# Starting the parts of x and the later tiles 64 bytes off the weights in each SBUF partition

## The chip, the cores and the metric

The kernel runs on one core of a Trainium2 chip. The metric is the device time of one execution in microseconds. The kernel before took 2917.8 us (median of 3 runs, 2917.19 to 2920.89).

## The reference, cut to what matters

The reference is a float32 transformer of two stacks of two layers on 512 tokens of 1024 features. Each layer mixes tokens in its own way, and most of the arithmetic is the dense products around the mixing:

```python
def first_block(x, mem, ...):
    for layer in range(DEPTH):            # 2
        mix = even_mixer(x, ...) or odd_mixer(x, ...)   # mLSTM + neighbourhood attention, differential attention
        x = layer_norm(DEEPNORM_ALPHA * x + mix, ...)
        xa = memory_cross_attention(x, mem, ...)        # 256 memory tokens
        x = layer_norm(DEEPNORM_ALPHA * x + xa, ...)
        ff = swiglu(x, ffn_w_gu[layer], ffn_w_down[layer])
        x = layer_norm(DEEPNORM_ALPHA * x + ff, ...)
    return x
```

The second stack has two more layers of mixer (HGRN2 and forgetting attention, RG-LRU and stick-breaking attention), layer norm, SwiGLU, layer norm. The hidden width of a SwiGLU is 2816.

## The kernel before

x is kept feature-major: 8 tiles of 128 features by 512 tokens. Every dense product is done in float32 accuracy with single-pass `float32r` matmuls: each operand is cut into a high and a low part that add up to it, and the product is the sum of three matmuls (high by high, low by high, high by low), `mm3`, lines 274 to 276. A matmul of TensorE has a stationary operand of 128 by 128, which a LDWEIGHTS brings in, and a moving operand whose columns stream past it. In this kernel every matmul has a weight load of its own.

`fetch` (from line 327) loads a block of weights of 128 by 1024 into `w_raw`, and ScalarE (line 337) and VectorE (line 339) make `w_hi` and `w_lo` of it. `block_a` multiplies such a block, as stationary operand, with the parts of x (`xh`, `xl`) or of the hidden units (`f_h`, `f_l`) as moving operand, 512 or 256 columns wide. `proj_b` does it the other way round: the parts of x are stationary and 512 columns of the weights move. `close_sublayer` ends a sublayer in two halves of 256 tokens, so its matmuls are 256 columns wide, and it keeps four of its eight blocks of weights in a pool of its own, `cw`. `mem_kv` makes keys and values of the memory: for the keys the parts of the memory (`mm_h`, `mm_l`, 256 columns) move past the weights, for the values 512 columns of the weights move past the parts of the memory.

The order of the instructions on each engine is set by the program and its scheduler. Where a tile lies is set by pools: a pool opened later begins where the one before it ends, each tile behind the other, in bytes of each of the 128 partitions; pools of the right side (those of the memory, `mem` and `kv`) grow from the top. The constants end with a tile of 16 bytes and with others that put everything behind them 32 bytes behind a multiple of 128; all big tiles are multiples of 128 bytes (most of 2048 or 4096), so that nearly everything on the left side begins at 32 (mod 128).

Of the kernel before, what the change touches and what calls it, by code (L numbers as in the profile page):

```python
# [8 lines left out]
F32 = mybir.dt.float32  # L9
# [7 lines left out]
P = 128  # L17
# [11 lines left out]
# last layer norm: tiles that GpSimd subtracts from and multiplies, that VectorE ends, and how they are stored  # L29
# [24 lines left out]
def layout(i):  # L54
    """Lays the inputs out for the loads of the program; values are copied, never changed."""
# [25 lines left out]
    # neighbourhood bias, per kind of query tile: [head, query, kind, key]; keys outside the window are shut out  # L81
# [125 lines left out]
class Prog:  # L207
    def __init__(self, ctx, tc, a):
        self.tc, self.nc, self.a = tc, tc.nc, a
        nc = tc.nc  # L210
        self.cp = ctx.enter_context(tc.tile_pool(name="cst", bufs=1))
        self.st = ctx.enter_context(tc.tile_pool(name="state", bufs=1))
        self.wp = ctx.enter_context(tc.tile_pool(name="wts", bufs=4))
        self.ps = ctx.enter_context(tc.tile_pool(name="ps", bufs=4, space=PSUM))
        st = self.st
        xf = st.tile([P, KT * S], F32, name="xf")
        self.XF = [xf[:, k * S : (k + 1) * S] for k in range(KT)]
        self.all_x = xf.rearrange("p (k s) -> p k s", k=KT)
        self.XH = [st.tile([P, S], F32R, name=f"xh{k}") for k in range(KT)]
        self.XL = [st.tile([P, S], F32R, name=f"xl{k}") for k in range(KT)]  # L220
        self.AO = [st.tile([P, S], F32, name=f"ao{k}") for k in range(KT)]
        cp = self.cp

        ones = cp.tile([P, 2 * P], F32, name="k_ones")
        nc.vector.memset(ones[:, 0:P], 1.0 / D)
        nc.vector.memset(ones[:, P : 2 * P], 1.0 / P)
        self.ones_d, self.ones_p = ones[:, 0:P], ones[:, P : 2 * P]
        nr = cp.tile([P, P], F32R, name="k_nr")
        nc.vector.tensor_scalar(nr, ones[:, P : 2 * P], -float(P), None, ALU.mult)
        self.mones_r = nr  # L230
        pr = cp.tile([P, P], F32R, name="k_pr")
        nc.vector.tensor_copy(pr, ones[:, P : 2 * P])
        self.ones_pr = pr
        cc = cp.tile([P, 4], F32, name="k_cc")
        nc.vector.memset(cc[:, 0:1], LN_EPS)
        nc.vector.memset(cc[:, 1:2], 1.0)
        self.eps, self.one = cc[:, 0:1], cc[:, 1:2]
        self.kv = {}
        self.pending = []
        self.biases = []  # L240
        self.before = []
        self.loaded = False
# [12 lines left out]
    def mm(self, tag="mm"):  # L255
        """A bank of PSUM: mm for projections, sc for scores, tp for what follows them."""
        return self.ps.tile([P, S], F32, name="p_" + tag, tag=tag, bufs={"mm": 2, "sc": 4, "tp": 2}[tag])
# [20 lines left out]
    def pair_parts(self, pool, name, width=S):  # L278
        """Room for the scores of two heads of 64 features, twice: per head q (both its parts over each
        other), the high part of k twice, and its low part beside zeros."""  # L280
        sets = []
        for b in range(2):
            q = [pool.tile([P, S], F32R, name=f"{name}q{b}{j}", bufs=1) for j in range(2)]
            k1 = [pool.tile([P, width], F32R, name=f"{name}h{b}{j}", bufs=1) for j in range(2)]
            k2 = [pool.tile([P, width], F32R, name=f"{name}l{b}{j}", bufs=1) for j in range(2)]
            sets.append((q, k1, k2))
        return sets

    def split_q(self, q, src, scale, view=lambda t: t, source=lambda t: t):
        """q[j] = both parts of scale * (rows of head j); the low one in the rows of the other head."""  # L290
# [9 lines left out]
    def split_k(self, k1, k2, pieces, clear, view=lambda t: t):  # L300
        """The parts of k; pieces: (columns, rows of the pair). clear: the zeros are still to be set."""
# [18 lines left out]
    def mm2(self, out, w, x, start, stop):  # L320
        """Sum of the products of all pairs of operands."""
        pairs = [(a, b) for a in w for b in x]
        for n, (a, b) in enumerate(pairs):
            self.nc.tensor.matmul(out, a, b, start=start and n == 0, stop=stop and n == len(pairs) - 1)  # L324

    def fetch(self, src, n=1024, pool=None):
        """Loads a block of weights and splits it into two parts that add up to it exactly."""
# [14 lines left out]
    def block_a(self, w, ps, xh, xl, c0=0, c1=S, kts=None):  # L342
        """ps[:, c0:c1] = (block of W)^T x for the 128 features of the block."""
# [5 lines left out]
    def proj_a(self, src, evac, halves=False, tags=("mm",)):  # L349
        """Feature-major products for a list of blocks; evac(n, psum, c0, c1)."""  # L350
# [20 lines left out]
    def settle(self, count=None):  # L371
        """What the sublayer before left to be done behind the first products of this one."""
        now = self.pending[:count]
        self.pending = self.pending[len(now) :]
        for f in now:
            f()

    def proj_b(self, src, lhs, ntile, evac, halves=False, banks=None):
        """Token-major products with 512 features; lhs(k, t) gives the parts of x^T of token tile t."""
# [31 lines left out]
    def close_sublayer(self, src, hs, ls, first, ln, last=False, keep=True):  # L411
        """x = layer_norm(alpha x + (rest of the sum)); src: 8 blocks, hs/ls: their inputs.
        keep: all of the blocks stay on chip for the second half of the tokens."""
# [4 lines left out]
        more_w = scope.enter_context(tc.tile_pool(name="cw", bufs=4, reuse_waits="tile")) if keep else None  # L418
        turn = dict.fromkeys("sqxrmt", 0)

        def room(kind):
            """A [128, 256] place in AO, which holds nothing at the end of a sublayer."""
# [5 lines left out]
        def statistics(sm, sq, more=()):  # L428
            """Means and reciprocals of the standard deviations, on all partitions."""
# [111 lines left out]
    def close_mixer(self, src, ln, keep=True):  # L541
        """Output projection of what lies in AO; its parts take the place of those of x."""
# [48 lines left out]
    def mem_kv(self, l, pool):  # L591
        """Keys (feature-major, in two parts) and values (token-major) of the memory."""
# [37 lines left out]
    def normalise(self, p, rs, n):  # L630
        """Divides the n score rows held side by side in p by their sums."""
# [5 lines left out]
    def in_turn(self, n, project, scores, values, between=None, place=0):  # L637
        """Work on n groups of heads, the products for the groups to come before what waits for a softmax.
        place: 0 projects one group ahead; 1 and 2 two groups, before the values or after the scores."""
# [94 lines left out]
    def conv_taps(self, out, xp, w, taps, bias=None):  # L734
        """out[t] = sum_j w[j] xp[t + j] (+ bias)."""
# [8 lines left out]
    def mlstm(self, tp, dp):  # L744
        nc, tc, a = self.nc, self.tc, self.a
        w = a["w_e1"]
        with ExitStack() as ctx:
# [36 lines left out]
            # log_sigmoid(f) = min(f, 0) - ln(1 + exp(-|f|)), its sums along each direction,  # L784
            # and the running maximum of log_i - sums
# [73 lines left out]
            def values(h, gs):  # L859
                hs = slice(h * P, h * P + P)  # L860
                for d in range(2):
                    num = self.mm("sc")
                    # g[i] covers the queries from tile i on, or up to it
# [55 lines left out]
    def neighbour(self, tp, between):  # L919
# [3 lines left out]
        def cr(t):  # L923
            """The tokens of a (row, column) grid, column by column."""
            return t.rearrange("p (r c) -> p c r", r=8)

        with tc.tile_pool(name="na", bufs=2, reuse_waits="tile") as np_:
# [64 lines left out]
            def values(pr, x):  # L992
                v, pp = x
                tabs = []
                for p in pp:
                    # key tiles: columns 0-7 and 56-63, 8-23, 24-39, 40-55
# [32 lines left out]
    def rms_rows(self, pool, o, g, out, gate=None):  # L1029
        """out = o / sqrt(mean over the 128 features of o^2 + eps) * g (* gate)."""  # L1030
# [133 lines left out]
    def hgrn(self, fill):  # L1164
        nc, tc, a = self.nc, self.tc, self.a
        w = a["w_e2"]
        with tc.tile_pool(name="hg", bufs=2, reuse_waits="tile") as hp:
# [11 lines left out]
            # lower bound of the forget gates: first row of the softmax over the layers  # L1179
# [34 lines left out]
            def factors(b, q, k, h):  # L1214
                """Left halves of the blocks of 2h tokens: k decayed up to the middle; right halves: q from there."""
# [18 lines left out]
            for h in range(4):  # L1234
# [14 lines left out]
                for n, hl in enumerate(LEVELS):  # L1249
# [11 lines left out]
                    # the queries are the right halves  # L1261
# [6 lines left out]
                # sums over whole blocks of 128, then 256 tokens for the blocks further off  # L1268
# [26 lines left out]
    def neg_log_sigmoid(self, t, tmp):  # L1295
        """t = ln(1 + exp(-|t|)) - min(t, 0)"""
# [7 lines left out]
    def fox_gates(self, pool, cd):  # L1304
        """Sums of -log(forget gate) over the tokens, per head."""
# [15 lines left out]
    def fox(self, v, cd):  # L1321
        nc, tc, a = self.nc, self.tc, self.a
        w = a["w_e2"]
        with tc.tile_pool(name="fx", bufs=2, reuse_waits="tile") as fp:
# [8 lines left out]
            def scores(pr, x):  # L1333
                q, k1, k2 = x
                pairs = []
                for hh in range(2):
# [5 lines left out]
                    for t in (3, 2, 1, 0):  # L1342
                        ts, n = slice(t * P, t * P + P), t * P + P
                        ps = self.mm("sc")
                        # later queries are done with these keys by now
# [49 lines left out]
    def lru(self):  # L1395
        nc, tc, a = self.nc, self.tc, self.a
        w = a["w_o2"]
        with tc.tile_pool(name="lr", bufs=2, reuse_waits="tile") as lp:
# [6 lines left out]
            # -8 softplus(-lam)  # L1405
# [33 lines left out]
            for n in range(4):  # L1439
                r, i, xc = rr[n], ii[n], xcs[n]  # L1440
                nc.vector.tensor_tensor(xc, xc, i, ALU.mult)
                # 1 - a^2 = tanh(-log a) (1 + a^2)
# [12 lines left out]
    def stick(self):  # L1455
        nc, tc, a = self.nc, self.tc, self.a
        w = a["w_o2"]
        with tc.tile_pool(name="sb", bufs=2, reuse_waits="tile") as sp_:
# [10 lines left out]
            def scores(pr, x):  # L1469
                q, k1, k2 = x  # L1470
                heads = []
                for hh in range(2):
                    ws, parts = {}, {}
                    for i in (3, 2, 1, 0):
# [5 lines left out]
                        # softplus(z) = max(z, 0) + ln(1 + exp(-|z|)), for the keys before the query  # L1480
# [17 lines left out]
            def sums(heads):  # L1498
                for ws, parts in heads:
                    for i in (3, 2, 1, 0):  # L1500
                        # less the sums of softplus over the keys from this one up to the query
# [29 lines left out]
def place_tables(nc):  # L1531
    """Loads, where ScalarE needs another table of functions, the one that serves longest."""
# [59 lines left out]
```

## Time and profile before

| what | value |
|---|---|
| median of 3 runs | 2917.8 us |
| profiled execution, span | 2916.1 us |
| TensorE matmul (PE) busy | 2848.7 us, 98% |
| weight loads (PEld) busy | 2415.8 us, 83% |
| VectorE (DVE) busy | 1697.9 us, 58% |
| ScalarE (ACT) busy | 1274.5 us, 44% |
| GpSimd (POOL) busy | 444.1 us, 15% |

The profiled execution's own time is its span. A matmul's duration in the trace goes from its start to the arrival of its last result, so neighbouring matmuls overlap in it; the time that a matmul costs is the distance from its start to the start of the next one. PEld runs beside PE.

### The profile page before, as it was taken

How to read it: one execution, taken by the hardware profiler on the slowest of the kernel's cores; microseconds unless marked ns; L12 is line 12 of the kernel's file. 1: busy time of each engine (PE TensorE's matmuls, PEld its weight loads, DVE VectorE, ACT ScalarE, POOL GpSimd, SP SyncE). 2: the span in 40 equal slices, each digit the busy share in tenths (PEclk: the TensorE clock that was granted, in tenths of full speed). 3: DMA queues.
4: the chain of work that ended last, by engine and by line, in shares of the span. 5: the costliest groups of instructions: out<-in, count | busy, mean ns of one | idle time of the engine just before them, and what ended most of it. 6: DMA issues, size and time to landing. Idle time of an engine off the chain costs nothing.

```text
span 2916.1 us, 40036 instructions
## 1 busy us (share of the span) xinstructions
PE 2848.7 (98%) x15354; PEld 2415.8 (83%) x15354; DVE 1697.9 (58%) x3148; ACT 1274.5 (44%) x2328; POOL 444.1 (15%) x516
## 2 busy tenths in 40 slices
PE   9979999999999999999999999999999999999998
PEld 7668989888887678898888987798888977988887
DVE  5877756333368888563333767873333769733335
ACT  4545544222356776442222544652222548532223
POOL 0432112000031112030000333230000302300003
PEclk9999999999999999999999999999999999999999
DMA  5232522333233225233332321223332331133331
GB/s 180 76 102 84 160 73 73 101 92 97 88 110 92 66 74 173 59 90 99 94 102 76 110 68 59 87 80 101 95 95 90 94 93 43 59 101 99 96 94 67
DMA packets 83073, 269.08 MB, mean 92 GB/s; under 512 B 10649, under 2 KB 15145, under 8 KB 82881
## 3 DMA queue, kind: packets, MB, share of 16 engines
q1 hardware_dynamic: 81376, 261.49, 29.1%
q0 software_dynamic: 1504, 5.04, 0.5%
q8 instruction: 120, 1.97, 0.3%
q14 instruction: 73, 0.59, 0.1%
HBM read 260.14 MB, written 2.15 MB: 90 GB/s over the span
## 4 chain that ended last, share of the span: by engine, by line
PE 78%; DVE 14%; ACT 4%; issue 3%; DMA 1%; POOL 0%; SPq 0%; DVEq 0%; ACTq 0%; POOLq 0%
PE p_mm L275 14%; PE p_mm L274 13%; PE p_mm L276 13%; PE p_sc L274 10%; PE p_sc L276 10%; PE p_sc L275 9%; DVE w_lo L339 2%; DVE ao L450 2%; PE p_tp L275 1%; PE p_tp L274 1%; PE p_tp L276 1%; DVE ac L742 1%; DVE xl L460 1%; PE p_sc L324 1%; PE p_sc L1254 1%
## 5 line engine op out<-in xcount | busy, mean ns | idle before, releaser
L337 ACT ACTIVATE w_hi<-w_raw 128x1024 fp32r<-128x1024 f32 (+2 forms) x478 | 492.9, 1036 | 1107.7 <-PE p_mm L275 482.5
L339 DVE TENSOR_TENSOR w_lo<-w_raw,w_hi 128x512 fp32r<-128x512 f32 (+2 forms) x956 | 654.2, 713 | 507.6 <-ACT w_hi L337 501.3
L274 PE MATMUL p_mm<-xh,w_hi 128*128 128x512 f32 (+1 forms) x1920 | 688.1, 359 | 7.4 <-ACT w_hi L337 5.0
L275 PE MATMUL p_mm<-xl,w_hi 128*128 128x512 f32 (+1 forms) x1920 | 687.3, 358 | 5.9 <-DVE xl L460 4.0
L276 PE MATMUL p_mm<-xh,w_lo 128*128 128x512 f32 (+1 forms) x1920 | 682.9, 356 | 0.0
L275 PEld LDWEIGHTS p_mm<-xl,w_hi 128*128 128x128 f32 x1920 | 364.6, 190 | 59.4 <-DVE xl L460 6.7
L274 PEld LDWEIGHTS p_mm<-xh,w_hi 128*128 128x128 f32 x1920 | 364.6, 190 | 58.5 <-ACT w_hi L337 5.0
L276 PEld LDWEIGHTS p_mm<-xh,w_lo 128*128 128x128 f32 x1920 | 364.5, 190 | 49.4 <-issue 0.6
L274 PE MATMUL p_sc<-xh,w_hi 128*128 128x512 f32 (+1 forms) x1024 | 359.4, 351 | 0.0
L276 PE MATMUL p_sc<-xh,w_lo 128*128 128x512 f32 (+1 forms) x1024 | 358.6, 350 | 0.8 <-DVE w_lo L339 0.8
L275 PE MATMUL p_sc<-xl,w_hi 128*128 128x512 f32 (+1 forms) x1024 | 358.1, 350 | 0.0
L496 POOL TENSOR_TENSOR ao<-xf 128x256 f32<-128x256 f32 x20 | 19.9, 995 | 1689.0 <-DVE xf L489 1293.9
L568 DVE TENSOR_TENSOR f_s<-f_s,p_sc 128x512 f32<-128x512 f32 x80 | 55.0, 687 | 288.8 <-PE p_sc L276 288.8
L276 PEld LDWEIGHTS p_sc<-xh,w_lo 128*128 128x128 f32 x1024 | 193.7, 189 | 26.2 <-DVE w_lo L339 1.0
L274 PEld LDWEIGHTS p_sc<-xh,w_hi 128*128 128x128 f32 x1024 | 193.7, 189 | 25.7 <-issue 0.4
L275 PEld LDWEIGHTS p_sc<-xl,w_hi 128*128 128x128 f32 x1024 | 193.7, 189 | 25.5 <-issue 0.2
L274 PE MATMUL p_sc<-f_h,w_hi 128*128 128x512 f32 (+1 forms) x464 | 157.5, 339 | 0.0
L276 PE MATMUL p_sc<-f_h,w_lo 128*128 128x512 f32 (+1 forms) x464 | 157.2, 339 | 0.2
L275 PE MATMUL p_mm<-f_l,w_hi 128*128 128x512 f32 (+1 forms) x464 | 157.2, 339 | 0.0
L276 PE MATMUL p_mm<-f_h,w_lo 128*128 128x512 f32 (+1 forms) x464 | 156.8, 338 | 0.0
L274 PE MATMUL p_mm<-f_h,w_hi 128*128 128x512 f32 (+1 forms) x464 | 156.8, 338 | 0.0
L275 PE MATMUL p_sc<-f_l,w_hi 128*128 128x512 f32 (+1 forms) x464 | 156.7, 338 | 0.0
(435 smaller groups left out, 4721.9 us busy)
## 6 DMA issues: line engine op xcount, KB each, us to landing
w_raw<-in_f_gu SPq DMA_DIRECT2D x176, 512.0 KB, 3.5
w_raw<-in_w_e SPq DMA_DIRECT2D x70, 512.0 KB, 3.5
w_raw<-in_w_x SPq DMA_DIRECT2D x64, 512.0 KB, 3.8
w_raw<-in_w_o SPq DMA_DIRECT2D x64, 512.0 KB, 3.7
w_raw<-in_f_d SPq DMA_DIRECT2D x64, 448.0 KB, 3.3
w_raw<-in_f_d SPq DMA_DIRECT2D x32, 512.0 KB, 3.5
r_s<-r_t SPq DMA_DIRECT2D x64, 64.0 KB, 2.0
na_b<-in_na_bias SPq DMA_DIRECT2D x6, 384.0 KB, 2.9
```

What stands on the lines that cost most here:

```text
L274: nc.tensor.matmul(out, wh, xh, start=start, stop=False)
L275: nc.tensor.matmul(out, wh, xl, start=False, stop=False)
L276: self.last = nc.tensor.matmul(out, wl, xh, start=False, stop=stop)
L324: self.nc.tensor.matmul(out, a, b, start=start and n == 0, stop=stop and n == len(pairs) - 1)
L337: nc.scalar.activation(hi[:, :n], raw[:, :n], AF.Copy)
L339: nc.vector.tensor_tensor(lo[:, c], raw[:, c], hi[:, c].bitcast(F32), ALU.subtract)
L450: nc.vector.scalar_tensor_tensor(t, t, g, r, ALU.mult, ALU.mult)
L460: nc.vector.scalar_tensor_tensor(xl, t, b, xh.bitcast(F32), ALU.add, ALU.subtract)
L496: eng.tensor_tensor(sm, self.XF[order[0]][:, c], self.XF[m][:, c], ALU.add)
L568: nc.vector.tensor_tensor(s[:, c], s[:, c], ps[:, c], ALU.mult)
L742: nc.vector.scalar_tensor_tensor(out, xp[:, j : j + S], w[j], out, ALU.mult, ALU.add)
L1254: nc.tensor.matmul(ps[:, c * 64 : c * 64 + 64].rearrange("p (n h) -> p n h", h=hl), x[:, cs], halves(x[:, cs], hl)[1], start=True, stop=True,)
```

## The change

Four tiles of 64 bytes that nothing reads or writes are put between others; besides, comments and docstrings are taken out, which moves the line numbers. Cut to its core:

```diff
         self.wp = ctx.enter_context(tc.tile_pool(name="wts", bufs=4))
         self.ps = ctx.enter_context(tc.tile_pool(name="ps", bufs=4, space=PSUM))
+        ctx.enter_context(tc.tile_pool(name="off", bufs=1)).tile([P, 16], F32, name="pad_p")
         st = self.st
         xf = st.tile([P, KT * S], F32, name="xf")
...
+        st.tile([P, 16], F32, name="pad_x")
         self.XH = [st.tile([P, S], F32R, name=f"xh{k}") for k in range(KT)]
         self.XL = [st.tile([P, S], F32R, name=f"xl{k}") for k in range(KT)]
         self.AO = [st.tile([P, S], F32, name=f"ao{k}") for k in range(KT)]
+        st.tile([P, 16], F32, name="pad_w")
...
         more_w = scope.enter_context(tc.tile_pool(name="cw", bufs=4, reuse_waits="tile")) if keep else None
+        if more_w:
+            more_w.tile([P, 16], F32, name="pad_cw", bufs=1)
```

The instructions, their operands and their order on each engine stay as they are. Two waits are added, both on VectorE for an earlier instruction of VectorE itself, before the first `w_lo` of the two closes behind the memory attention. What changes is where tiles begin in each partition:

| tiles | start mod 128, before | after | start mod 256, before | after |
|---|---|---|---|---|
| `w_raw`, `w_hi`, `w_lo` in the common pool | 32 | 32 | 32 | 160 |
| `w_hi`, `w_lo` in `cw` | 32 | 32 | 32 | 32 |
| `xf` (x itself) | 32 | 32 | 32 | 32 |
| `xh`, `xl`, `ao` | 32 | 96 | 32 | 96 |
| `f_h`, `f_l`, `f_s` of the SwiGLU | 32 | 96 | 32 | 224 |
| `x_qh`, `x_ql` of the memory attention | 32 | 96 | 32 | 224 |
| `mm_h`, `mm_l`, `m_kh`, `m_kl` of the memory | 96 | 96 | 224 | 224 |

A slice of 128 or 256 columns begins 512 or 1024 bytes further, so the phase mod 256 of a tile holds for all its slices. The tiles of the mixers move by 64 among themselves and together.

## Rows read from the trace of the kernel before

**Rows 1.** The page: busy time, granted clock and chain of waits by engine.
```profile
PE 2848.7 (98%) x15354; PEld 2415.8 (83%) x15354; DVE 1697.9 (58%) x3148; ACT 1274.5 (44%) x2328; POOL 444.1 (15%) x516
...
PEclk9999999999999999999999999999999999999999
...
PE 78%; DVE 14%; ACT 4%; issue 3%; DMA 1%; POOL 0%; SPq 0%; DVEq 0%; ACTq 0%; POOLq 0%
```

**Rows 2.** Timeline, PE alone, SwiGLU: start us, us, engine, line, operation.
```profile
600.09 0.39 PE L274 MATMUL p_mm<-xh,w_hi 128*128 128x512 f32 x1
...
605.53 0.39 PE L274 MATMUL p_sc<-xh,w_hi 128*128 128x512 f32 x1
```

**Rows 3.** Timeline, PE alone, last part of a SwiGLU, 256 columns.
```profile
800.04 0.28 PE L274 MATMUL p_sc<-f_h,w_hi 128*128 128x256 f32 x1
...
803.64 0.28 PE L274 MATMUL p_sc<-f_h,w_hi 128*128 128x256 f32 x1
```

**Rows 4.** Timeline, PE alone, at the lowered clock; then windows: stretch, busy, clock.
```profile
1661.03 0.41 PE L274 MATMUL p_mm<-xh,w_hi 128*128 128x256 f32 x1
...
1662.95 0.41 PE L274 MATMUL p_mm<-xh,w_hi 128*128 128x256 f32 x1
...
1661.00:1662.40 1.40, 1.40 (x9) 1.40 (x8) 0.45 (x1) 0.80 (x3) 0.00 (x0) 0.50 0.00 0
```

**Rows 5.** Timeline, all engines: a weight load beside the matmul ahead of it.
```profile
1000.84 0.39 PE L274 MATMUL p_mm<-xh,w_hi 128*128 128x512 f32 x1
1000.85 0.19 PEld L275 LDWEIGHTS p_mm<-xl,w_hi 128*128 128x128 f32 x1
1001.07 0.39 PE L275 MATMUL p_mm<-xl,w_hi 128*128 128x512 f32 x1
```

**Rows 6.** Timeline, PE alone, keys of the memory, first layer.
```profile
316.02 0.28 PE L274 MATMUL p_sc<-mm_h,w_hi 128*128 128x256 f32 x1
...
320.78 0.28 PE L274 MATMUL p_mm<-mm_h,w_hi 128*128 128x256 f32 x1
```

**Rows 7.** Timeline, PE alone, keys of the memory, second layer.
```profile
1123.90 0.28 PE L274 MATMUL p_mm<-mm_h,w_hi 128*128 128x256 f32 x1
...
1126.73 0.28 PE L274 MATMUL p_sc<-mm_h,w_hi 128*128 128x256 f32 x1
```

**Rows 8.** Timeline, PE alone, values of the memory, first layer.
```profile
340.06 0.39 PE L274 MATMUL p_tp<-w_hi,mm_h 128*128 128x512 f32 x1
...
343.49 0.39 PE L274 MATMUL p_tp<-w_hi,mm_h 128*128 128x512 f32 x1
```

**Rows 9.** Groups by line and form, PE: count, busy us, mean ns from start to last result.
```profile
L274 PE MATMUL p_mm<-xh,w_hi 128*128 128x512 f32 x1280 | 503.8, 394 | 7.0 <-ACT w_hi L337 5.0 <-DVE nq L296 1.7 <-DVE sv L1460 0.3
...
L274 PE MATMUL p_sc<-xh,w_hi 128*128 128x512 f32 x640 | 249.0, 389 | 0.0
...
L274 PE MATMUL p_mm<-xh,w_hi 128*128 128x256 f32 x640 | 184.3, 289 | 0.4 <-ACT xh L264 0.2
...
L274 PE MATMUL p_sc<-xh,w_hi 128*128 128x256 f32 x384 | 110.4, 288 | 0.0
...
L274 PE MATMUL p_mm<-f_h,w_hi 128*128 128x512 f32 x240 | 93.4, 389 | 0.0
...
L274 PE MATMUL p_sc<-f_h,w_hi 128*128 128x256 f32 x224 | 64.1, 286 | 0.0
...
L274 PE MATMUL p_tp<-xh,w_hi 128*128 128x256 f32 x192 | 54.4, 283 | 0.0
...
L274 PE MATMUL p_mm<-w_hi,xh 128*128 128x512 f32 x96 | 38.4, 400 | 0.0
...
L274 PE MATMUL p_sc<-m_kh,x_qh 128*128 128x256 f32 x64 | 18.7, 293 | 0.0
```

**Rows 10.** Windows: stretch, busy us of PE, PEld, DVE, ACT and POOL, clock, DMA.
```profile
600.00:700.00 100.00, 100.00 (x443) 82.83 (x442) 36.00 (x58) 26.72 (x34) 0.00 (x0) 1.00 0.30 95
...
1000.00:1100.00 100.00, 94.15 (x549) 75.68 (x548) 86.00 (x164) 71.55 (x152) 21.36 (x20) 1.00 0.25 75
```

**Rows 11.** Groups by line and form, VectorE.
```profile
L449 DVE TENSOR_TENSOR ao<-xf,ao 128x256 f32<-128x256 f32 x107 | 57.2, 550 | 1.2 <-ACT ao L438 1.1
...
L500 DVE TENSOR_TENSOR ao<-ao,ao 128x256 f32<-128x256 f32 x19 | 8.0, 420 | 0.8
```

**Rows 12.** Timeline, PE alone: the first matmuls of the kernel.
```profile
8.49 0.40 PE L276 MATMUL p_tp<-xh,w_lo 128*128 128x512 f32 x1
...
10.56 0.39 PE L276 MATMUL p_mm<-xh,w_lo 128*128 128x512 f32 x1
```

## Prediction

> **What bounds the kernel now.** The page comes first: TensorE is busy 98% of the span, and 78% of the chain that ended last is its own [rows 1]. The clock is at its upper level (2.4 GHz) nearly throughout. So the question is what one matmul costs, and that is read as a distance between starts, for which the timeline of PE alone is the next view. In the SwiGLU 24 matmuls of 512 columns go by in 605.53 - 600.09 = 5.44 us, 226.7 ns each [rows 2]. At one column per cycle of 2.4 GHz 512 columns are 213.3 ns, so 13.3 ns (32 cycles) are lost in each. With 256 columns 30 matmuls take 3.60 us, 120.0 ns each [rows 3], against 106.7 ns: again 13.3 ns. The loss does not grow with the columns. It is there at the upper clock only: where the granted clock is 0.50 (1.2 GHz), 9 matmuls of 256 columns take 1.92 us, 213.3 ns each, exactly one column per cycle [rows 4]. A fixed number of cycles between two matmuls would have shown there too. What lies beside the stream of a matmul is the weight load of the next one, which begins 10 ns after the matmul does [rows 5]. I take the loss to be the two reads of SBUF getting into each other's way, which the slower clock leaves room for. That is an inference; the rows show only the loss.
>
> Does the place of the tiles matter? The kernel before already has matmuls whose two operands lie 64 bytes (mod 128) apart, those of the memory, with parts at 96 and weights at 32. For the keys (the memory's parts move) 42 matmuls in the first layer take 4.76 us, 113.3 ns each [rows 6], and in the second layer 24 take 2.83 us, 117.9 ns [rows 7]: the same code at the same addresses, in two states, both below the 120.0 ns of operands at the same phase. For the values (512 columns of the weights move, the memory's parts are stationary) 15 matmuls take 3.43 us, 228.7 ns each [rows 8], which is 2.0 ns above the 226.7. So distance changes the loss, to 6.7, 11.2 or 15.4 ns, and has done so in both directions.
>
> By the Trainium skill's page "SBUF — State Buffer", section "SBUF: two separate sides", only the port pair shared by VectorE and GpSimd causes contention on the engines' side, and TensorE never waits for anyone; by that rule start addresses would change nothing and the sum would be zero. Rows 6 and 7 beside rows 3 speak against it as far as 256 columns go.
>
> **The change part by part.** No instruction is added, removed or moved. The two added waits on VectorE are for its own work of a whole output block before, which is done by then; behind each stands the `w_lo` of a block that TensorE needs only after other blocks, so I cost them at nothing; without that cover they are two times some 0.2 us. DMAs write to `w_raw` and `xf`, whose phases stay.
>
> What is moved is the distance between moving and stationary operand, from 0 to 64 (mod 128), in these matmuls, each line of the groups standing for the three of `mm3` [rows 9]:
> - parts of x moving, 512 columns: 3 x (1280 + 640) = 5760; hidden units, 512 columns: 3 x 240 for `p_mm` and as many for `p_sc`, 1440; together 7200.
> - 256 columns: x 3 x (640 + 384 + 192) = 3648; hidden units 6 x 224 = 1344; together 4992.
> - weights moving past x, 512 columns: 6 x 96 = 576.
>
> The loss in all of them is 12,768 x 13.3 ns = 170 us, the most that could ever come back.
>
> For the 12,192 with activations moving, the nearest rows are the keys: the same roles, the same phases (96 moving, 32 stationary). They had both states, so I take the middle, 115.6 ns, 4.4 ns less than now, and since the loss is now equal at both widths I carry the 4.4 ns over to 512 columns. That last step no row shows; the bounds for it are -6.7 ns [rows 6] and +2.0 ns [rows 8].
> - 7200 x -4.4 = -31.7 us; 4992 x -4.4 = -22.0 us.
> - The 576 with moving weights have the values' roles: 576 x +2.0 = +1.2 us.
> - Scores of the memory attention, where keys and queries lay 64 apart and now lie together: 3 x 64 matmuls, x +4.4 = +0.8 us.
>
> Sum -51.7 us of TensorE's time. Not all of it is on the path: in the SwiGLU TensorE has no idle time at all, in the attention of the odd layer it stands at 94% while VectorE works 86% [rows 10]; a faster TensorE waits more there. I count 90%: -46.5 us. On the profiled execution's own 2916.1 us this gives 2869.6; the median of the runs shown is 1.7 us above that execution, so 2871.
>
> VectorE: `ao<-xf,ao`, 107 times, gets inputs 64 apart where they lay together. The trace has 550 ns for it and 420 ns for a like operation on two places of `ao` [rows 11]; if phases made all that difference, either way, it would be 107 x 0.13 = 14 us of VectorE, of which little is on the chain. I take nothing, as VectorE's two reads are one operation's and the 130 ns can be anything. What is late next in the attentions is VectorE's and ScalarE's work on weights and scores, unchanged in size.
>
> **The rivals.**
> 1. *No effect.* The keys run faster for another reason (their tiles of 256 columns, the right side). For it: the rule of the page named above, and that the values got nothing. Against it: the two widths lose the same 13.3 ns everywhere else, in 256 columns of x and of hidden units alike. Time 2917.8.
> 2. *The width decides.* 256 columns gain as the keys did, 512 columns lose as the values did: 4992 x -4.4 + 7776 x +2.0 + 0.8 = -5.6 us, 2913; with the keys' two states from -17 to +6 us (2901 to 2924).
> 3. *The distance counts over 256 bytes, not 128.* Keys lay 192 (mod 256) ahead of their weights, values' weights 64 ahead. After the change x is 192 ahead of the common pool's weights, hidden units only 64; in the closes with `cw` it is the reverse for those blocks. Then 5760 x -4.4 = -25.3, 1440 x +2.0 = +2.9, 576 x +2.0 = +1.2; of the 256 columns about two thirds gain (3270 x -4.4 = -14.4), a third loses (1620 x +2.0 = +3.2), the keys lose their own gain (384 x 6 = +2.3). Sum -30 us, nine tenths of it -27: 2891.
> 4. *Slower.* The reads at 64 apart settle into a state with more loss than the one at 0, which is itself a settled one: the first matmuls of the kernel at the upper clock take 2.07 us for 9, 230.0 ns [rows 12], before they come down to 226.7. If both widths stand where the values stand, 12,768 x +2.0 = +25.5 us, nine tenths 23: 2941; if they stay at the unsettled 230.0, +3.3 ns, 38 us: 2956. Against it: the keys, in both layers. It decides where 512 columns lose more than the 22 us that 256 columns gain, that is from 229.5 ns a matmul on.
>
> **How the numbers follow.** My forecast (both widths gain) 0.50, with 2847 if all take the better state (12,192 x -6.7 + 2 = -80, nine tenths -72) and 2897 if all take the worse (12,192 x -2.1 + 2 = -24, nine tenths -21). Distance over 256 bytes 0.14, width decides 0.12, no effect 0.13, slower 0.11. A measurement here tells 0.2% (5.8 us) from no change: faster than 2912 are the first two and a half of the width's case, 0.70; within it no effect and a third of the width's case, 0.16; slower the rest, 0.14. The range goes from 2840 (a little more than the better state everywhere) to 2920 (no effect); it leaves out the slower case and tails, under 2 in 10. The forecast's own range is 2847 to 2897.
>
> **What would show it.** In the timeline of the SwiGLU a distance of 220.0 or 224.5 ns in place of 226.7, and in its last part 113 to 118 in place of 120.0, would show the main step right; 226.7 unchanged, rival 1; 228.7 at 512 beside 113 to 118 at 256, rival 2; x gaining and `f_h` losing, rival 3. The scores of the memory attention should come to 120. The idle time of PE in the attentions should grow by some 5 us. The forecast is wrong where 512 columns do not go below 226, since they carry three fifths of the sum.

## The result and the profile after

The changed kernel takes 2942.3 us (median of five runs, 2940.0 to 2943.0) against 2917.8: a ratio of 1.0076 with a 95% interval of 1.0064 to 1.0088, slower by 24.5 us. I had forecast 2871 with a range of 2840 to 2920; neither held.

The page of the changed kernel, where [rows 1] stand for before: busy time, granted clock, and the chain of waits by engine.

```profile
span 2938.8 us, 40036 instructions
...
PE 2870.6 (98%) x15354; PEld 2397.2 (82%) x15354; DVE 1694.3 (58%) x3148; ACT 1274.0 (43%) x2328; POOL 443.6 (15%) x516
...
PEclk9999999999999999999999999999999999999999
...
PE 78%; DVE 13%; ACT 4%; issue 3%; DMA 1%; POOL 1%; SPq 0%; DVEq 0%; ACTq 0%; POOLq 0%
```

The span grew by 22.7 us, TensorE's busy time by 21.9 (2848.7 to 2870.6). The counts of instructions are the same; VectorE, ScalarE and GpSimd are as busy as before within 4 us. `ao<-xf,ao` on VectorE, whose two reads now lie 64 bytes apart, takes 551 ns where [rows 11] have 550. So the time is TensorE's own, and the next view is the distance between starts.

The timeline of the changed kernel, PE alone (start us, us, engine, line, operation; a matmul starts every 0.11 to 0.23 us, and those left out run at the same pace): the values of the memory, x of a SwiGLU, its hidden units with 512 columns, and with 256.

```profile
337.79 0.39 PE L278 MATMUL p_mm<-w_hi,mm_h 128*128 128x512 f32 x1
...
349.69 0.39 PE L278 MATMUL p_tp<-w_hi,mm_h 128*128 128x512 f32 x1
...
604.08 0.39 PE L278 MATMUL p_mm<-xh,w_hi 128*128 128x512 f32 x1
...
608.98 0.40 PE L278 MATMUL p_sc<-xh,w_hi 128*128 128x512 f32 x1
...
701.01 0.39 PE L278 MATMUL p_mm<-f_h,w_hi 128*128 128x512 f32 x1
...
703.07 0.39 PE L278 MATMUL p_mm<-f_h,w_hi 128*128 128x512 f32 x1
...
804.85 0.28 PE L278 MATMUL p_mm<-f_h,w_hi 128*128 128x256 f32 x1
...
808.74 0.28 PE L278 MATMUL p_sc<-f_h,w_hi 128*128 128x256 f32 x1
```

- x, 512 columns: 21 matmuls in 4.90 us, 233.3 ns each; [rows 2] have 226.7.
- Hidden units, 512 columns: 9 in 2.06 us, 228.9 ns.
- Hidden units, 256 columns: 33 in 3.89 us, 117.9 ns; [rows 3] have 120.0. This stretch stands in the worse of the two states of [rows 6] and [rows 7]; over the whole trace x with 256 columns averages 114.8 ns and the hidden units 115.3, some two thirds of the stretches near 113.3 and one third near 117.8.
- Values: 51 in 11.90 us, 233.3 ns; [rows 8] have 228.7. Here too only the distance changed.

The groups by line and form (count, busy us, mean ns from start to last result), where [rows 9] stand for before:

```profile
L278 PE MATMUL p_mm<-xh,w_hi 128*128 128x512 f32 x1280 | 511.1, 399 | 6.7 <-ACT w_hi L341 4.9 <-DVE nq L300 1.7
...
L278 PE MATMUL p_sc<-xh,w_hi 128*128 128x512 f32 x640 | 253.1, 396 | 0.0
...
L278 PE MATMUL p_mm<-xh,w_hi 128*128 128x256 f32 x640 | 181.0, 284 | 0.6 <-ACT xh L268 0.5
```

Each form moves by about what its pace moved: +5 to +7 ns with 512 columns, -5 ns with 256.

For the whole kernel I lined the starts of all matmuls up with those of before and summed the differences of their distances. A distance that is under 1.15 times the median of its form in both traces counts as pace, any other as a wait; that limit is my choice. Pace with 512 columns gives +40.1 us, pace with 256 columns -22.1, waits at 256 columns +6.9, waits at 512 columns -2.3, all else +0.2: together +22.8, against +22.7 in the span.

### The profile page after: what moved, and what is told of

It reads as the page before. It is cut to its first block, busy times and chain, and to the rows that moved or that the text cites. A ratio compares the mean times of both kernels' runs of the same rounds, so it can differ in the third digit from the quotient of the medians.

```text
span 2938.8 us, 40036 instructions
## 1 busy us (share of the span) xinstructions
PE 2870.6 (98%) x15354; PEld 2397.2 (82%) x15354; DVE 1694.3 (58%) x3148; ACT 1274.0 (43%) x2328; POOL 443.6 (15%) x516
## 4 chain that ended last, share of the span: by engine, by line
PE 78%; DVE 13%; ACT 4%; issue 3%; DMA 1%; POOL 1%; SPq 0%; DVEq 0%; ACTq 0%; POOLq 0%
PE p_mm L279 14%; PE p_mm L278 13%; PE p_mm L280 13%; PE p_sc L278 9%; PE p_sc L280 9%; PE p_sc L279 9%; DVE w_lo L343 2%; DVE ao L456 2%; PE p_tp L279 1%; PE p_tp L280 1%; PE p_tp L278 1%; DVE xl L466 1%; DVE ac L748 1%; DVE ao L455 1%; PE p_sc L328 1%
```

## The experiments

Two questions: what in the distance between the operands decides, and does TensorE do this alone? The main theory (W) is that distance mod 256 and width decide together, in TensorE itself; its rivals are that other engines' reads and writes beside it decide (U), that the weight load beside the stream makes a loss in proportion to its size (L), that the loss is a fixed one (F), and that only the distance mod 128 counts. "Distance" is the start of the moving operand less that of the stationary one, in bytes of a partition, mod 256. Rows give starts to 0.01 us, so a pace over nine matmuls is known to about 1 ns. A ratio compares a run with the kernel before as executed beside it, whose medians were 2919.8 to 2922.5 us.

**bench_moving, bench_stationary.** The network is replaced by rows of matmuls in groups of three, as `mm3` issues them. In the first the moving operand is shifted, in the second the stationary one. The code, cut to its core and moved to the left:

```diff
+for t in range(PER):
+    k = t % 8
+    for q, (w, m) in enumerate(((WH, M0), (WH, M1), (WL, M0))):
+        mo, wo = (e, 0) if moved else (0, e)   # e: the shift in columns of 4 bytes
+        nc.tensor.matmul(ps[:, 0:width], w[:, wo + k * P : wo + k * P + P], m[:, mo : mo + width],
+                         start=t == 0 and q == 0, stop=t == PER - 1 and q == 2)
```

> Leaves the whole network out; what is left is rows of matmuls in the order of the three of `mm3`, moving operand shifted by 0 to 240 bytes against the stationary one in steps of 16, at 512 and 256 columns, and by 0, 64, 128, 192 at 384, 448 and 128 columns, with ScalarE, GpSimd and the DMA queues idle and VectorE all but idle. Theory W (distance and width together set the loss, TensorE alone): 512 columns 226.7 ns at 0, about 229 at 64, about 233 at 192; 256 columns 120.0 at 0, 113 to 118 at 64 and 192. Rival U (the loss needs the traffic of the other engines, and the change only moved that): one figure per width at every distance, near 213.3 ns for 512 and 106.7 ns for 256 columns.

> Also leaves the network out: the same matmuls, but the stationary operand is shifted by 0 to 224 bytes in steps of 32, the moving one stays. Theory W, if only the distance (moving minus stationary, mod 256) counts: a shift of 64 here gives what 192 gives in the run with the moving operand shifted (512 columns about 233 ns, 256 columns 113 to 118), a shift of 192 what 64 gives there (229 ns; 113 to 118). If the own phase of an operand counts, the two tables differ. Rival U: flat again.

The timeline of bench_moving, PE alone: 512 columns at distance 0, 64 and 192, then 256 columns at 0 and 64.

```profile
45.16 0.39 PE L1596 MATMUL p_b<-m,wl 128*128 128x512 f32 x1
...
46.52 0.39 PE L1596 MATMUL p_b<-m,wl 128*128 128x512 f32 x1
...
95.31 0.39 PE L1596 MATMUL p_b<-m,wl 128*128 128x512 f32 x1
...
97.37 0.40 PE L1596 MATMUL p_b<-m,wl 128*128 128x512 f32 x1
...
197.49 0.40 PE L1596 MATMUL p_b<-m,wl 128*128 128x512 f32 x1
...
200.29 0.40 PE L1596 MATMUL p_b<-m,wl 128*128 128x512 f32 x1
...
244.12 0.28 PE L1596 MATMUL p_b<-m,wl 128*128 128x256 f32 x1
...
245.56 0.28 PE L1596 MATMUL p_b<-m,wl 128*128 128x256 f32 x1
...
269.99 0.28 PE L1596 MATMUL p_b<-m,wl 128*128 128x256 f32 x1
...
271.76 0.28 PE L1596 MATMUL p_b<-m,wl 128*128 128x256 f32 x1
```

512 columns: 6 in 1.36 us (226.7 ns), 9 in 2.06 (228.9), 12 in 2.80 (233.3). 256 columns: 12 in 1.44 (120.0), 15 in 1.77 (118.0). The timeline of bench_stationary, PE alone, 512 columns with the stationary operand shifted by 64, which is distance 192:

```profile
100.67 0.39 PE L1596 MATMUL p_b<-m,wl 128*128 128x512 f32 x1
...
103.47 0.39 PE L1596 MATMUL p_b<-m,wl 128*128 128x512 f32 x1
```

12 in 2.80 us, 233.3 ns again. These are the paces of the two kernels, in a program whose page has VectorE busy 2%, ScalarE 1% and GpSimd 0%. U falls. The paces by distance, in ns, worked out from both traces (two figures: the pace was one in one row of matmuls and the other in another):

| distance | 0 | 32 | 64 | 96 | 128 | 160 | 192 | 224 |
|---|---|---|---|---|---|---|---|---|
| 512, moving shifted | 226.7 | 233.3 | 228.9 | 233.3 | 232 | 234 | 233.3 | 233.4 |
| 512, stationary shifted | 226.7 | 233.2 | 228.9 | 233.3 | 232-233.8 | 234 | 233.6 | 233.5 |

| distance | 0 | 64 | 192 |
|---|---|---|---|
| 256, moving shifted | 120.0 | 117.8, 113.2 | 117.8, 113.3 |
| 256, stationary shifted | 120.0 | 117.8 | 117.8, 113.3 |

It does not matter which operand is shifted. With 512 columns distance 0 is the best of the 16 tried (240 had 226.7 in one row of matmuls, 233.3 and 236.8 in the others); with 256 columns it is about the worst. 113.3 and 117.8 occur at one address and one distance, as in [rows 6] and [rows 7].

**bench_load.** The same as bench_moving at distances up to 448, and with stationary operands of 64 and 32 columns in place of 128 (against bench_moving, cut to its core):

```diff
-ps[:, 0:width], w[:, wo + k * P : wo + k * P + P], m[:, mo : mo + width],
+ps[0:wide, 0:width], w[:, k * P : k * P + wide], m[:, e : e + width],
```

> Leaves the network out, as the two rows of matmuls before it: now the stationary operand is also 64 and 32 columns wide (a half and a quarter of the weight load), at distances 0, 64 and 192, and for 128 columns the distance goes on from 256 to 448 bytes. If the loss comes from the weight load's reads beside the moving operand's (theory L), it shrinks with the load: from 13.3 ns at distance 0 to about 7 and 3 at 512 columns, and the differences between distances with it. If it is a fixed price of a change of stationary operand (theory F), it stays 13.3 ns. Distances of 256, 320, 448 give what 0, 64, 192 give (226.7, 228.9, 233.3; 120.0, 113 to 118, 113 to 118) if the pattern repeats every 256 bytes; if it repeats every 512, they differ.

The timeline of bench_load, PE alone: stationary operand of 32 columns, 512 columns moving, distance 64, then 192; stationary operand of 64 columns, 256 moving, distance 0, then 192; the whole operand of 128, 512 moving, distance 320.

```profile
142.12 0.40 PE L1595 MATMUL p_b<-m,wl 128*32 128x512 f32 x1
...
144.21 0.39 PE L1595 MATMUL p_b<-m,wl 128*32 128x512 f32 x1
...
163.87 0.39 PE L1595 MATMUL p_b<-m,wl 128*32 128x512 f32 x1
...
166.65 0.39 PE L1595 MATMUL p_b<-m,wl 128*32 128x512 f32 x1
...
190.23 0.28 PE L1595 MATMUL p_b<-m,wl 128*64 128x256 f32 x1
...
191.93 0.28 PE L1595 MATMUL p_b<-m,wl 128*64 128x256 f32 x1
...
212.25 0.28 PE L1595 MATMUL p_b<-m,wl 128*64 128x256 f32 x1
...
214.75 0.28 PE L1595 MATMUL p_b<-m,wl 128*64 128x256 f32 x1
...
280.75 0.39 PE L1595 MATMUL p_b<-m,wl 128*128 128x512 f32 x1
...
282.81 0.39 PE L1595 MATMUL p_b<-m,wl 128*128 128x512 f32 x1
```

With 512 columns, 9 in 2.09 us (232 ns) and 12 in 2.78 (231.7); at distance 0 it is 231.7 too. A quarter of the load does not make the loss smaller (18.4 ns over the 213.3 of one column per cycle, where the full load at distance 0 loses 13.3), so L falls as a proportion; but the distance no longer matters, so the size of the stationary operand does take part. (It sets the load and the number of result rows at once, so that it acts through the load is argued, not shown.) A fixed 13.3 ns (F) is not right either: with 64 columns it was 230.0 at distance 0, 228.3 at 64 and 232 at 192.

With 256 columns the smaller operands turn the order over: 64 columns gave 113.3 ns at distance 0 (15 in 1.70 us; one row of four had 120.0), 116.7 at 64 and 119.0 at 192 (21 in 2.50), and 32 columns gave 113.3 to 117.8 at all three. So there distance 0 is the best, where with the whole operand it is about the worst.

At 320 the whole operand has 9 in 2.06 us. Distances 256, 320, 384 and 448 gave 226.7, 228.9, 232.7 and 233.3: the table repeats after 256 bytes, not after 128.

**narrow64.** Before, with the weights of the 256-column passes alone begun 64 bytes later (distance 192); 512 columns stay at 0.

```diff
+NARROW, WIDE = 16, 0  # columns by which the parts of the weights begin later
-        hi = pool.tile([P, 1024], F32R, name="w_hi", tag="w_hi", bufs=4)
+        hi = pool.tile([P, 1088], F32R, name="w_hi", tag="w_hi", bufs=4)[:, off : off + 1024]
...
-        ws = [self.fetch(s) for s in src]
+        ws = [self.fetch(s, off=NARROW) for s in src]
```

> The kernel before, but the parts of the weights of the 256-column passes (first blocks of a sublayer, both halves of its end) begin 64 bytes later than those of the 512-column passes, inside somewhat larger tiles; x and all else as before. Theory W: 512 columns stay at 226.7 ns, 256 columns go from 120.0 to 113 to 118 ns; in the changed kernel the starts of the 256-column groups drew together by 18 us in all, so 2917.8 - 18 to 26 = 2892 to 2900. Rival U: no better than the changed kernel's direction, 2917 to 2942.

The timeline of narrow64, PE alone: x with 512 columns, hidden units with 256.

```profile
603.84 0.39 PE L275 MATMUL p_sc<-xh,w_hi 128*128 128x512 f32 x1
...
605.88 0.39 PE L275 MATMUL p_sc<-xh,w_hi 128*128 128x512 f32 x1
...
798.91 0.28 PE L275 MATMUL p_sc<-f_h,w_hi 128*128 128x256 f32 x1
...
805.27 0.28 PE L275 MATMUL p_mm<-f_h,w_hi 128*128 128x256 f32 x1
```

2909.6 us, ratio 0.9964 (0.9952 to 0.9977): faster. 512 columns stay at 226.7 (9 in 2.04), 256 come down to 117.8 (54 in 6.36). The sign was as expected, the size was not: mostly the worse of the two states, -16.9 us of pace at 256 columns, and 7.1 us of waits there in return.

**wide64.** The converse: `NARROW, WIDE = 0, 16`, so that 512 columns alone are at distance 192 (against narrow64):

```diff
-NARROW, WIDE = 16, 0  # columns by which the parts of the weights begin later
+NARROW, WIDE = 0, 16  # columns by which the parts of the weights begin later
```

> The converse: the parts of the weights begin 64 bytes later in the 512-column passes, and at the old place in the 256-column passes. Theory W: 7200 matmuls of 512 columns at 233.3 ns (+6.6) = +47.5 us, 576 with moving weights at 229 = +1.3 us, 256 columns unchanged; some nine tenths on the path, 2917.8 + 44 = 2962, slower than the changed kernel. Rival U: between before and the changed kernel, 2918 to 2942.

The timeline of wide64, PE alone: hidden units, 512 columns, which were at distance 64 in the changed kernel.

```profile
604.49 0.39 PE L275 MATMUL p_sc<-f_h,w_hi 128*128 128x512 f32 x1
...
606.59 0.40 PE L275 MATMUL p_sc<-f_h,w_hi 128*128 128x512 f32 x1
```

2961.1 us, ratio 1.0146 (1.0130 to 1.0161), and the hidden units at 233.3 too (9 in 2.10 us); 256 columns stay at 119.8. So at one and the same distance, 192, the 256 columns alone gain (narrow64) and the 512 columns alone lose: there the width decides the sign.

**plus64.** The changed kernel with its pads ahead of the weights made 192 bytes, so that x and hidden units lie at 64 from all weights, where they had some at 192 and some at 64. By a period of 128 bytes nothing changes.

```diff
-        st.tile([P, 16], F32, name="pad_w")
+        st.tile([P, 48], F32, name="pad_w")
...
-            more_w.tile([P, 16], F32, name="pad_cw", bufs=1)
+            more_w.tile([P, 48], F32, name="pad_cw", bufs=1)
```

> The changed kernel with two of its four pads enlarged from 64 to 192 bytes, so that parts of x and hidden units lie 64 bytes ahead of all weights (mod 256) in place of 192; mod 128 nothing changes. If only the distance mod 128 counts, 2942 as the changed kernel. If it counts mod 256: 7200 matmuls of 512 columns at 228.9 (+2.2) = +16, 576 with moving weights at 233.3 (+6.6) = +4, 4992 of 256 columns at 117.8 (-2.2) = -11, of which a third is lost in waits: 2917.8 + 16 + 4 - 7 = 2930.

The timeline of plus64, PE alone: x with 512 columns, hidden units with 256.

```profile
603.61 0.39 PE L278 MATMUL p_mm<-xh,w_hi 128*128 128x512 f32 x1
...
605.67 0.39 PE L278 MATMUL p_mm<-xh,w_hi 128*128 128x512 f32 x1
...
799.77 0.28 PE L279 MATMUL p_sc<-f_l,w_hi 128*128 128x256 f32 x1
...
804.36 0.28 PE L279 MATMUL p_sc<-f_l,w_hi 128*128 128x256 f32 x1
```

2931.2 us, ratio 1.0038 (1.0026 to 1.0051), as expected of 256 bytes: x at 228.9 (9 in 2.06 us), while the weights that move past x went the other way, from 229.1 to 233.3; 256 columns at 117.7 (39 in 4.59).

**narrow144.** narrow64 with 36 columns (144 bytes, distance 112), where the bench had 113.3 to 115.3 ns.

```diff
-NARROW, WIDE = 16, 0  # columns by which the parts of the weights begin later
+NARROW, WIDE = 36, 0  # columns by which the parts of the weights begin later
```

> As the kernel with only the weights of the 256-column passes shifted, but by 144 bytes, so that the moving operand is 112 ahead (mod 256), where the row of matmuls gave 114.8, 115.3 and 113.3 ns against 113.2 to 117.8 at 64 and 192. If that carries over, 2 ns less than in the shift by 64 (116 to 117 ns) for 4992 matmuls = -10 us, two thirds of it on the path: 2903. If the state is a matter of chance at any distance, 2906 to 2912.

The timeline of narrow144, PE alone, hidden units with 256 columns.

```profile
801.88 0.28 PE L275 MATMUL p_sc<-f_h,w_hi 128*128 128x256 f32 x1
...
805.12 0.28 PE L275 MATMUL p_sc<-f_h,w_hi 128*128 128x256 f32 x1
```

A miss: 2919.2 us, ratio 0.9993 (0.9984 to 1.0002), with 120.0 ns at 256 columns (27 in 3.24 us). Ten of the eleven executions took 2916.9 to 2920.7; one took 2910.8, and no trace of it is there to say why. The bench's figure at a distance that is no multiple of 64 did not carry over. There the moving operand had left the multiples of 64, here the stationary one; I did not try these apart.

**bench_width.** Other widths between 256 and 512 columns, at distances 0, 64 and 192.

```diff
+PLAN = ((512, (0, 0), 128),) + tuple((n, (0, 64, 192), 128) for n in (512, 496, 480, 464, 448, 416, 384, 352, 320, 288, 272, 264, 256, 504))
```

> Leaves the network out: the rows of matmuls again, at 14 widths from 256 to 512 columns and the distances 0, 64 and 192. Theory W says that the width decides what a distance does, without saying how. If the gain at 64 apart is one of narrow matmuls, whose weight load takes up the whole matmul, the loss at 64 falls below that at 0 from some width downwards and stays there (one crossing between 512 and 256). If it is a matter of how the length of a matmul falls on some period, the better distance changes back and forth with the width; 448 columns (200.0 at 64 against 206.7 at 0) and 384 (173.3 at both) already hint at that.

Ten of the fourteen widths, in ns (two figures, or a range, where the rows of matmuls differed):

| columns | 512 | 504 | 480 | 464 | 448 | 416 | 384 | 320 | 272 | 256 |
|---|---|---|---|---|---|---|---|---|---|---|
| 0 | 226.7 | 226.7 | 216.7 | 208.9 | 202.6, 206.7 | 186.7-188.3 | 173.3 | 146.7 | 125.5 | 120.0 |
| 64 | 228.9 | 228.9 | 218.3 | 210.0 | 200.0 | 188.3 | 173.3 | 146.7 | 126.7 | 117.8 |
| 192 | 233.3 | 228.9 | 216 | 213.3 | 202.2 | 186.7 | 174.9 | 146.7 | 123.3 | 117.8, 113.3 |

There is no one width at which the sign turns: distance 0 is best at 512, level with 192 at 480, ahead at 464, behind at 448, level at 320, behind distance 192 at 272. So no rule "short streams gain" holds; the figures are facts about each width. At distance 0 the loss over one column per cycle isn't the same everywhere either: 13.3 ns at 512, 384 and 256 columns, but 16 to 20 at 448 and 12 at 272.

**bench_parts.** The three matmuls of a group share operands; here the moving high part, the moving low part and the stationary low part each get a distance of their own, 64 combinations for either width.

```diff
+for q, (w, m, wo, mo) in enumerate(((WH, M0, 0, dh // 4), (WH, M1, 0, dl // 4), (WL, M0, wl // 4, dh // 4))):
```

> Leaves the network out: 512 and 256 columns, with distances of their own (0, 64, 128, 192) for the high part of the moving operand, its low part, and the low part of the stationary one against its high part, 64 combinations each. If each matmul's loss depends only on its own pair (moving operand, next stationary one), 512 columns are best at 0, 0, 0 with 226.7 ns and every other combination is a mean of 226.7 to 233.3; 256 columns at best 113.3. If matmuls behind each other matter together, some combination goes below 226.7, towards 220.

With 512 columns all at 0 stays best (226.7; the next combinations have 228.9, the worst 235.6). With 256 columns two combinations gave 113.3 ns both times: (64, 64, 128) and (192, 192, 128), moving parts and low weights counted from the high weights; with the low weights not shifted, (192, 192, 0) had 117.8 and 113.3. The combinations aren't the means of what their pairs have alone: in (0, 64, 64) each stream is at distance 0 from the next stationary operand, which alone would give 226.7 at 512 columns, and it had 231.1 and 232.5. So the matmuls next to each other matter together; yet no combination went below 226.7, which the expectation had asked of that case.

**narrow_split.** narrow64 with high weights 64 and low weights 192 bytes later, which is (192, 192, 128).

```diff
-NARROW, WIDE = 16, 0  # columns by which the parts of the weights begin later
+NARROW, WIDE = (16, 48), (0, 0)  # columns by which the high and the low part of the weights begin later
```

> As the kernel with only the weights of the 256-column passes shifted, but their high part begins 64 bytes and their low part 192 bytes behind the old place, the best of the 64 combinations in the row of matmuls (113.3 ns both times, where the plain shift by 64 stood at 117.8 or 113.3). If the row carries over, 256 columns at 113.3 ns in nearly all of the 4992, 6.7 ns less than before = -33 us; of the 19.5 us by which the plain shift shortened them the span got 7.5 to 9, so here some half: 2917.8 - 16 = 2902. If the state is not kept in the kernel (as with the shift by 144), 2909, as the plain shift, or worse.

The timeline of narrow_split, PE alone, hidden units with 256 columns.

```profile
801.29 0.28 PE L275 MATMUL p_sc<-f_h,w_hi 128*128 128x256 f32 x1
...
804.69 0.28 PE L275 MATMUL p_sc<-f_h,w_hi 128*128 128x256 f32 x1
```

2904.6 us, ratio 0.9942 (0.9929 to 0.9956), close to what was expected: 113.3 ns (30 in 3.40 us), the better state nearly throughout (x with 256 columns averages 113.9), and 512 columns at 226.7. It beats both kernels. (The 19.5 us of narrow64 in the expectation are 16.9 by the count used here.)

Its gain of pace is 28.9 us at 256 columns, of which 12.2 come back as waits there. Where some of them are, the waits of PE say (waiting matmul, line, what it waits for: us in total, times, longest us). In the kernel before:

```profile
PE p_sc L435 <- DVE ao L499: 3.9, 3, 1.4
...
PE p_mm L275 <- POOL xl L463: 1.7, 2, 0.8
```

In the changed kernel, the same two:

```profile
PE p_sc L441 <- DVE ao L505: 5.8, 5, 2.4
...
PE p_mm L279 <- POOL xl L469: 3.6, 8, 0.8
```

In narrow_split:

```profile
PE p_sc L436 <- DVE ao L500: 7.8, 5, 2.4
...
PE p_mm L276 <- POOL xl L464: 3.7, 8, 0.8
```

At the closes of the sublayers TensorE arrives earlier at what VectorE and GpSimd still have to finish. The two rows show 3.8 us more for the changed kernel and 5.9 for narrow_split, about half of what the distances say at 256 columns. The page's idle time of PE hardly moves (67.4 to 68.2 us from before to after), since it counts a matmul as busy to its modelled end, 0.28 us after a start that the next one follows within 0.12. The rest of the waits I did not place.

## Why the prediction was wrong

- **The step that failed** is "since the loss is now equal at both widths I carry the 4.4 ns over to 512 columns", the term 7200 x -4.4 = -31.7 us. Measured: +6.6 ns for the 5760 with x and +2.2 for the 1440 with hidden units, 5760 x 6.6 + 1440 x 2.2 = +41 us; the traces have +40.1 of pace at 512 columns, moving weights included. Equal losses at distance 0 said nothing of the losses at other distances, and bench_width shows that even the equality was one of these two widths: at 448 columns the loss at distance 0 is 16 to 20 ns. wide64 and narrow64 show the two signs apart.
- **The bounds were no bounds.** I had +2.0 ns [rows 8] as the worst at 512 columns. Those rows stand at distance 64, most of the changed matmuls at 192, where the bench has +6.6. Keys and values differed in width, in distance and in roles at once; I ascribed the difference to the roles, and bench_stationary and the values after the change (233.3) show that it was width and distance.
- **256 columns** were right: forecast -22.0 us, pace measured -22.1, by the keys' two states as read from [rows 6] and [rows 7]. That the size fits so well is in part luck: I took half of each state, the trace has about two thirds of the better one, and plus64, with all of them at distance 64, mostly the worse (117.3 on average); nothing here says what chooses. I had counted 90% of the gain as on the path; 6.9 of the 22.1 came back as waits, so about 70% stayed.
- **Small terms.** The 576 with moving weights stand at 229.1 ns (+2.4; forecast +2.0). The scores of the memory attention, now at distance 0, stand at 118.9 (forecast 120). The keys and values of the memory, which I put at nothing since their distance mod 128 stays, changed places mod 256: the 384 matmuls of the keys went from 192 to 64 and from 115.7 to 117.6 ns on average, the 192 of the values from 64 to 192 and from 229.1 to 233.3, together some 1.5 us more. VectorE's `ao` did not change. The added waits show no cost: TensorE waits 1.4 us for `w_lo` in the kernel before and 1.3 in the changed one.
- **The rivals.** "The width decides" had the right signs, but with +2.0 for all of 512 columns it came to 2913. "Distance over 256 bytes" had the period right (plus64, bench_load) and the sign at 192 wrong for 512 columns and at 64 wrong for 256. The measured time is their combination: +40.1 of pace at 512 columns, -22.1 at 256 and +4.8 of waits and the rest are the 22.8 us by which the trace grew. "Slower" gave 2941, nearly the time, from a mechanism that isn't this one: there both widths lost 2 ns. Its point of decision, 229.5 ns at 512 columns, was the right thing to watch, and x went past it.
- **The rule weighed.** "No effect" is refuted. By the Trainium skill's page "SBUF — State Buffer", section "SBUF: two separate sides", TensorE never waits on anyone at SBUF. No run here shows it waiting for another engine there: in bench_moving, with the others all but idle, the paces are those of the kernels. But there and in the changed kernel a matmul slowed from 226.7 to 233.3 ns by its start address alone, so the zero that I had worked out from the rule does not follow. The measurement decides.
- **What stays open.** That the stream and the weight load get into each other's way in SBUF remains an inference: with a quarter of the stationary operand the distance stops mattering at 512 columns, but the loss does not shrink, and with a half of it distance 0 becomes the best at 256. Why distance 0 is best at 512 columns and about the worst at 256 with the whole operand, what chooses between 113.3 and 117.8 ns, and why distance 112 did not carry over are not settled.

## What to carry to other kernels

Where TensorE is the bound, a start address is worth some per cent of a matmul, with a sign that depends on the width: measure it in a bench of the kernel's own group of matmuls, at each width and each distance over 256 bytes, and check it in the kernel, since not every figure carries over. Place the operands for each use, not by one offset for all: here 512 columns want distance 0, 256 columns want the split one. Two rows that differ in three things can't bound a third case.

## What the hardware showed that I had not expected

- Distance counts over 256 bytes: 64 and 192 differ by 4.4 ns at 512 columns (228.9 and 233.3), 64 and 320 don't.
- With 128 columns a matmul starts every 111.3 to 112.0 ns at every distance, hardly sooner than with 256 columns in their better state (113.3).
- The same code at the same addresses has two paces at 256 columns, 113.3 and 117.8 ns; with moving parts at 64 or 192 and the low weights 128 bytes off the high ones nearly only the better one was seen.
- A smaller stationary operand did not make a matmul of 512 columns faster: 226.7 ns with 128 columns, 230.0 with 64, 231.7 with 32, at distance 0. One of 256 columns it did: 120.0 with 128, 113.3 with 64 in three rows of four.
